# Four seed loads of ple_gate's second product, moved in the SyncE queue from six pieces ahead of their use to just behind the loads of its first blocks

## The chip, the cores and the metric

The kernel runs on one core of one Trainium2 chip. The metric is the time of one execution on the device, in microseconds (us). Before the change it is 787.4 us, the median of three runs (786.9 to 788.35 us). The times of single instructions below come from one further execution, taken by the hardware profiler.

## The reference

One layer of a transformer trunk, in float32: a windowed attention with a gate, an output projection, a gated embedding, and a norm. With DEPTH = 1 only the first of four mixers runs. In the words of the reference, shortened:

```python
hn = rmsnorm(x, norm_g[0])                      # x is 512 x 2048
q, k, v, gate = split(hn @ w_in)                # widths 2048, 256, 256, 2048
scores = q k^T / 8 + bias, masked to a window of 128
probs = softmax(scores with one sink for each head)
y = ((probs @ v) * silu(gate)) @ w_out          # 2048 x 2048
x = x + y
emb = p[0] @ ple_proj[0]                        # 256 -> 2048
g = sigmoid(rmsnorm(x, ple_norm[0]) @ ple_gate[0])   # 2048 x 2048
x = x + emb * g
return rmsnorm(x, final_g)
```

## The kernel before

**Number format.** Each float32 operand is split into a high part, rounded to the format float32r, and a low part, the rest. A product is three matmuls: high times high, high times low, low times high (lines 126 to 128, `mm3`).

**Stages.** Up to about 451 us the kernel makes q, k, v, the gates and the attention. Then come two products with a 2048 x 2048 matrix each: `w_out`, and after it `ple_gate`, from about 621 us on. Each is done as a scheme of Strassen's kind: six large products of half-sized blocks, in the order 1, 7, 6, 5, 3, 4 (`ORDER_PLE`), and a seventh, number 2, done one level deeper as seven small products that are put between the pieces of the large ones. Some of these products take sums of weight blocks. For the numbers 7 and 5 of `ple_gate` such sums were written to HBM during the attention, and they are loaded from there.

**Pieces.** All weights of the two products come as a list of pieces (`Pieces`, line 725), 128 x 1024 in float32, 512 KB each, numbered in the order in which TensorE uses them. Piece 71 is the first of `ple_gate`. Its product 1 takes the pieces 71 to 74 (first half) and 75, 76, 78, 79 (second half), with the small pieces 77 and 80 between them. Its second product, number 7, takes the pieces 81, 82, 84, 85 (first half) and 88, 90, 92, 93 (second half), with the small pieces 83, 86, 87, 89, 91 and 94 between them. TensorE needs 12 matmuls for a large piece and 6 for a small one. A step here means the work on one piece.

**Kinds of pieces.** The eight pieces of product 7 are *seeds*: each is loaded into one of eight tiles named `grown`. Product 6 uses these tiles after another block was added to each by an accumulating DMA on the GpSimd queue (line 739), and product 4 uses them after a second such addition. An addition to a tile is issued when the tile was split for the product before. All other pieces are loaded by SyncE (line 752) into tiles named `braw`, whose rooms are: the eight `grown` rooms for the pieces from `w_out`'s product 6 to its end (piece 70), then three rooms `wraw` and one `fourth`, taken in turns. A room comes free when its piece was split.

**Split and use.** A piece is split by ScalarE (line 760, `bhi`) and VectorE (line 761, `blo`), two steps ahead of its use, into three rooms for the split parts. So the split of a piece waits until TensorE is done with the piece three before, and it waits for the piece's load.

**The order of loads.** TensorE and SyncE run in the order in which the program is written. At step i, `ahead` (line 774) issues the load of each piece that may be loaded up to there: three ahead for `braw` before piece 71, five ahead where they take `grown` rooms, four ahead from step 71 on, and six ahead for a seed:

```python
for n in range(max(i, 0), min(i + 6, last) + 1):
    kind = self.specs[n][0]
    if n not in self.base and n >= self.done and kind not in ("grow", "emb") and (kind == "seed" or n <= i + (...)):
        self._prepare(n)
```

If a load has to wait for its room, all that SyncE has behind it waits too.

**Turning x.** Between the two products x is turned, for a part by DMAs on the GpSimd queue: `turn_blocks` writes blocks to HBM (`apart<-blocks`, line 1064), `gather_blocks` reads them back (`s<-apart`, line 1072), and ScalarE scales what came back (`hT`, line 1081).

Of the kernel before, what the change touches and what calls it, by code (L numbers as in the profile page):

```python
# [55 lines left out]
def trunk_kernel(ctx: ExitStack, tc: tile.TileContext, a: dict):  # L56
# [31 lines left out]
    class Weights:  # L88


        def __init__(self, ahead):
            self.srcs, self.ahead, self.raw, self.made = [], ahead, [], []

            self.todo, self.asked, self.apart = [], 0, False
# [104 lines left out]
    for k in range(KC):  # L199
# [45 lines left out]
        if k == 0:  # L245
            first, second = slice(0, 1), slice(1, 2)
# [154 lines left out]
    for b in range(exact, BUCKETS):  # L401
        d = np.nonzero(bk == b)[0]
        if len(d):
            lo, n = P - 1 + int(d.min()), len(d)
# [281 lines left out]
    def block(nm, r, c, jj, m):  # L686

        r = r if nm == "w_out" else 3 - r
        return a[nm][2 * (c - 1) + jj, 4 * (r - 1) + m]
# [35 lines left out]
    class Pieces:  # L725
# [48 lines left out]
        def ahead(self, i):  # L774

            last = len(self.specs) - 9
            for n in range(max(i, 0), min(i + 6, last) + 1):
                kind = self.specs[n][0]
                if n not in self.base and n >= self.done and kind not in ("grow", "emb") and (kind == "seed" or n <= i + (5 if far_from <= n < far_to else 4 if i >= far_to else 3)):
                    self._prepare(n)  # L780
            while self.done <= min(i + 2, last):
                self._split(self.done)
                self.done += 1
# [14 lines left out]
    B = Pieces()  # L798

    def add_stage(nm, order):  # L800
        at = {}

        for p in order:
            for jj in range(2):
                at[p, jj] = []
                for m in range(4):
                    at[p, jj].append(len(B.specs))
                    if (nm, p) in SUMS:
                        src = summed[nm, p, jj, m]
                    else:  # L810
                        src = block(nm, *{1: (1, 1), 3: (2, 2), 6: (1, 1), 4: (2, 1)}[p], jj, m)
                    growing = () if nm == "w_out" else (7, 6, 4)
                    kind = "one" if p not in growing else "seed" if p == growing[0] else "grow"
                    B.add(kind, src, (nm, jj, m) if p in growing else None)
                    if nm == "w_out" and (p, jj, m) in EMBED_AT:
                        at.setdefault("embed", []).append(len(B.specs))
                        B.add("emb", None)
                    for q in SMALL[nm].get((p, jj), {}).get(m, ()):
                        v = at.setdefault(("small", q), [])
                        src = summed.get(("small", nm, q, len(v)))  # L820
                        if src is None:
                            src = small_block(nm, *{1: (1, 1), 2: (2, 1), 3: (2, 2)}[q], len(v))
                        v.append(len(B.specs))
                        B.add("one", src)
        return at
# [8 lines left out]
    at_out = add_stage("w_out", ORDER_OUT)  # L834
    at_ple = add_stage("ple_gate", ORDER_PLE)

    far_from, far_to = at_out[6, 0][0], at_ple[ORDER_PLE[0], 0][0]

    class Forms:
# [850 lines left out]
    first = block(0, 0)  # L1690
# [44 lines left out]
    n = done[3]  # L1735
# [81 lines left out]
```

## Time and profile before

| what | before |
|---|---|
| median of three runs | 787.4 us (786.9 to 788.35) |
| time of the profiled execution | 788.12 us |
| its span, first to last instruction | 786.4 us |
| TensorE (PE) busy | 774.0 us, 98% of the span |
| VectorE (DVE) busy | 617.8 us, 79% |
| ScalarE (ACT) busy | 528.5 us, 67% |
| DMA queue q1 (SyncE's loads) | 154.58 MB, 56.1% of 16 engines |
| DMA queue q0 (GpSimd's, with the additions) | 57.74 MB, 35.0% |

Times inside the span count from its start. In a timeline row the first number is the start, the second the duration, and what stands in brackets is the engine's idle time before and what ended it. `SPq` is SyncE issuing a DMA. In a row of DMA issues, the last number is the median time from issue to landing. Matmul starts follow each other every 0.227 us when nothing is in the way, and their ends overlap, so starts are compared and not ends. In a row of a window, the columns are the length, then busy time and number of instructions of PE, PEld, DVE, ACT and POOL, then the granted TensorE clock, the busy share of the 16 DMA engines, and what they moved in GB/s.

### The profile page before, as it was taken

How to read it: one execution, taken by the hardware profiler on the slowest of the kernel's cores; microseconds unless marked ns; L12 is line 12 of the kernel's file. 1: busy time of each engine (PE TensorE's matmuls, PEld its weight loads, DVE VectorE, ACT ScalarE, POOL GpSimd, SP SyncE). 2: the span in 40 equal slices, each digit the busy share in tenths (PEclk: the TensorE clock that was granted, in tenths of full speed). 3: DMA queues.
4: the chain of work that ended last, by engine and by line, in shares of the span. 5: the costliest groups of instructions: out<-in, count | busy, mean ns of one | idle time of the engine just before them, and what ended most of it. 6: DMA issues, size and time to landing. Idle time of an engine off the chain costs nothing.

```text
span 786.4 us, 11143 instructions
## 1 busy us (share of the span) xinstructions
PE 774.0 (98%) x3652; PEld 645.6 (82%) x3652; DVE 617.8 (79%) x1069; ACT 528.5 (67%) x1121; POOL 167.2 (21%) x303
## 2 busy tenths in 40 slices
PE   9999999999999999999999999999999999999995
PEld 8888888888888888888888888888888888777884
DVE  4546697877877688877878899976899889878995
ACT  6643586766767676766666654678766888846974
POOL 0201523122222314132322200001111211221111
PEclk9999999999999999999999999999999999999998
DMA  9988899999999989999998589869799699999966
GB/s 347 291 209 298 184 276 303 293 279 269 278 257 271 270 240 287 267 293 256 290 255 206 142 319 329 274 208 309 260 366 335 210 354 287 276 279 282 328 145 215
DMA packets 52410, 213.02 MB, mean 271 GB/s; under 512 B 7984, under 2 KB 9008, under 8 KB 46592
## 3 DMA queue, kind: packets, MB, share of 16 engines
q1 hardware_dynamic: 39152, 154.58, 56.1%
q0 software_dynamic: 13200, 57.74, 35.0%
q8 instruction: 29, 0.48, 0.2%
q14 instruction: 29, 0.24, 0.1%
HBM read 195.45 MB, written 78.69 MB: 349 GB/s over the span
## 4 chain that ended last, share of the span: by engine, by line
PE 88%; DMA 4%; DVE 3%; issue 2%; ACT 2%; POOL 0%; POOLq 0%; DVEq 0%; ACTq 0%
PE gps L126 7%; PE gps L127 7%; PE gps L128 7%; PE qps L126 7%; PE qps L128 7%; PE qps L127 7%; PE o L128 6%; PE o L126 6%; PE o L127 6%; PE g L127 2%; PE s L485 2%; DMA braw<-in_ple_gate 2%; PE g L128 2%; PE g L126 2%; DMA braw<-ple_gate 2%
## 5 line engine op out<-in xcount | busy, mean ns | idle before, releaser
L761 DVE TENSOR_TENSOR blo<-braw,bhi 128x1024 fp32r<-128x1024 f32 x100 | 121.3, 1218 | 29.1 <-ACT bhi L760 28.3
L760 ACT CAST bhi<-braw 128x1024 fp32r<-128x1024 f32 x100 | 105.0, 1051 | 52.6 <-PE o L128 19.6
L126 PE MATMUL gps<-xh,whi 128*128 128x512 f32 x256 | 100.0, 390 | 0.0
L127 PE MATMUL gps<-xl,whi 128*128 128x512 f32 x256 | 100.0, 390 | 0.0
L128 PE MATMUL gps<-xh,wlo 128*128 128x512 f32 x256 | 99.8, 390 | 0.0
L126 PE MATMUL qps<-xh,whi 128*128 128x512 f32 x224 | 87.8, 392 | 0.0
L128 PE MATMUL qps<-xh,wlo 128*128 128x512 f32 x224 | 87.5, 390 | 0.0
L127 PE MATMUL qps<-xl,whi 128*128 128x512 f32 x224 | 87.4, 390 | 0.0
L575 POOL TENSOR_SCALAR_AFFINE_SELECT own<-r 64x512 fp32r<-64x512 f32 (+1 forms) x48 | 32.5, 677 | 238.4 <-DVE r L565 234.5
L110 DVE TENSOR_TENSOR wlo<-wraw,whi 128x1024 fp32r<-128x1024 f32 x60 | 73.5, 1226 | 3.2 <-ACT whi L109 3.1
L126 PE MATMUL o<-bhi,fho 128*128 128x512 f32 x192 | 74.8, 390 | 0.0
L127 PE MATMUL o<-blo,fho 128*128 128x512 f32 x192 | 74.7, 389 | 0.0
L128 PE MATMUL o<-bhi,flo 128*128 128x512 f32 x192 | 74.7, 389 | 0.0
L109 ACT CAST whi<-wraw 128x1024 fp32r<-128x1024 f32 x60 | 62.4, 1040 | 5.1 <-issue 4.1
L127 PE MATMUL g<-blo,fhg 128*128 128x512 f32 x160 | 63.5, 397 | 1.7 <-DVE blo L761 1.7
L126 PE MATMUL g<-bhi,fhg 128*128 128x512 f32 x160 | 63.1, 394 | 0.9 <-ACT bhi L760 0.9
L128 PE MATMUL g<-bhi,flg 128*128 128x512 f32 x160 | 62.9, 393 | 0.0
L128 PEld LDWEIGHTS gps<-xh,wlo 128*128 128x128 f32 x256 | 48.1, 188 | 10.2
L126 PEld LDWEIGHTS gps<-xh,whi 128*128 128x128 f32 x256 | 48.1, 188 | 9.2
L529 ACT ACTIVATE t<-t,sm 128x129 f32<-128x129 f32 (+1 forms) x128 | 49.6, 389 | 8.6 <-DVE sm L525 7.4
L127 PEld LDWEIGHTS gps<-xl,whi 128*128 128x128 f32 x256 | 48.1, 188 | 8.9
L564 ACT CAST r<-pt 128x256 fp32r<-128x256 f32 x56 | 20.9, 372 | 50.0 <-PE pt L551 49.5
(297 smaller groups left out, 1830.0 us busy)
## 6 DMA issues: line engine op xcount, KB each, us to landing
wraw<-in_w_gate_in SPq DMA_DIRECT2D x32, 512.0 KB, 8.1
w_out<-in_w_out POOLq DMA_DIRECT2D x32, 512.0 KB, 9.0
braw<-w_out SPq DMA_DIRECT2D x32, 512.0 KB, 6.1
wraw<-in_w_q SPq DMA_DIRECT2D x28, 512.0 KB, 6.5
braw<-in_w_out SPq DMA_DIRECT2D x22, 512.0 KB, 5.9
braw<-in_ple_gate SPq DMA_DIRECT2D x22, 512.0 KB, 6.4
xw<-in_first SPq DMA_DIRECT2D x14, 640.5 KB, 6.6
w_out<-in_w_out SPq DMA_DIRECT2D x16, 512.0 KB, 10.2
```

The source lines that it names most:

```text
L109: nc.scalar.copy(hi, raw)
L110: nc.vector.tensor_sub(lo, raw, hi.bitcast(F32))
L126: nc.tensor.matmul(ps, sh, mh, start=first, stop=False, skip_group_check=more)
L127: nc.tensor.matmul(ps, sh, ml, start=False, stop=False, skip_group_check=more)
L128: nc.tensor.matmul(ps, sl, mh, start=False, stop=last, skip_group_check=more)
L485: nc.tensor.matmul(s_ps[:, u, : 2 * n], st, of_keys[:, first * 2 * QB : (first * QB + n) * 2], start=True, stop=True)
L529: nc.scalar.activation(su, su, AF.Exp, bias=sm[:, u : u + 1], accum_out=sm[:, 2 + u : 3 + u])
L564: nc.scalar.copy(rh, src)
L575: nc.gpsimd.affine_select(out=flat(own), in_=flat(r).bitcast(F32), pattern=[[0, 8], [sign, HB]], compare_op=ALU.is_ge, fill=0.0, base=-HB ...
L760: nc.scalar.copy(hi[:, :n], raw)
L761: nc.vector.tensor_sub(lo[:, :n], raw, hi[:, :n].bitcast(F32))
```

## The change

Four of the eight seeds, the pieces 81, 82, 84 and 85, are now loaded at the steps 67, 68, 69 and 70, one at each. They were loaded at the steps 75, 76, 78 and 79. No load is added or removed, and every other engine's order stays as it was.

```diff
@@ Pieces.ahead @@
                 if n not in self.base and n >= self.done and kind not in ("grow", "emb") and (...):
                     self._prepare(n)
+            first = at_ple[ORDER_PLE[0], 0][0] - 4
+            if first <= i < first + 4 and seeds[i - first] not in self.base:
+                self._prepare(seeds[i - first])
             while self.done <= min(i + 2, last):
                 self._split(self.done)
                 self.done += 1
@@ after add_stage @@
     at_out = add_stage("w_out", ORDER_OUT)
     at_ple = add_stage("ple_gate", ORDER_PLE)
 
+    seeds = [n for n, (kind, _, _) in enumerate(B.specs) if kind == "seed"]
     far_from, far_to = at_out[6, 0][0], at_ple[ORDER_PLE[0], 0][0]
```

SyncE's queue at the end of `w_out`, before (the number behind `braw` or `grown` is the piece's; in brackets stand the semaphores it waits for, where DVE means that a split must have freed its room):

```order
L752 DMA braw70_6449<-w_out_4_1_3_811 128x1024 [waits DMAHW0_49,DVE_49]
L752 DMA braw71_6497<-in_ple_gate 128x1024 [waits DMAHW1_49]
L752 DMA braw72_6509<-in_ple_gate 128x1024 [waits DMAHW2_49,DVE_49]
L752 DMA braw73_6556<-in_ple_gate 128x1024 [waits DMAHW3_49]
L752 DMA braw74_6604<-in_ple_gate 128x1024 [waits DMAHW4_49]
L752 DMA braw75_6606<-in_ple_gate 128x1024 [waits DMAHW5_49,DMAHW1_49,DVE_49]
```

The same place in the changed kernel:

```order
L752 DMA braw70_6449<-w_out_4_1_3_811 128x1024 [waits DMAHW0_49,DVE_49]
L752 DMA grown81_6471<-ple_gate_7_0_0_814 128x1024 [waits DMAHW1_49,DVE_49]
L752 DMA braw71_6499<-in_ple_gate 128x1024 [waits DMAHW2_49]
L752 DMA grown82_6501<-ple_gate_7_0_1_815 128x1024 [waits DMAHW3_49,DVE_49]
L752 DMA braw72_6513<-in_ple_gate 128x1024 [waits DMAHW4_49]
L752 DMA grown84_6515<-ple_gate_7_0_2_816 128x1024 [waits DMAHW5_49,DVE_49]
L752 DMA braw73_6562<-in_ple_gate 128x1024 [waits DMAHW6_49]
L752 DMA grown85_6564<-ple_gate_7_0_3_817 128x1024 [waits DMAHW7_49,DVE_49]
L752 DMA braw74_6612<-in_ple_gate 128x1024 [waits DMAHW0_49]
L752 DMA braw75_6614<-in_ple_gate 128x1024 [waits DMAHW2_49,DMAHW1_49,DVE_49]
```

Each of the four seeds stands ahead of one of the pieces 71 to 74 and waits for a split: its room is that of piece 63, 64, 65 or 66.

SyncE's queue in `ple_gate`'s first product, before:

```order
L752 DMA braw79_6707<-in_ple_gate 128x1024 [waits DMAHW5_49,DVE_49]
L752 DMA grown81_6709<-ple_gate_7_0_0_814 128x1024
L752 DMA braw80_6739<-in_ple_gate 128x1024 [waits DMAHW6_49,DVE_49]
L752 DMA grown82_6741<-ple_gate_7_0_1_815 128x1024
L752 DMA grown84_6778<-ple_gate_7_0_2_816 128x1024
L752 DMA braw83_6809<-small_ple_gate_7_0_812 128x1024 [waits DMAHW7_49,DVE_49]
L752 DMA grown85_6811<-ple_gate_7_0_3_817 128x1024
L752 DMA braw86_6870<-small_ple_gate_7_1_813 128x1024 [waits DMAHW0_49,DVE_49]
L752 DMA grown88_6872<-ple_gate_7_1_0_818 128x1024 [waits DMAHW1_49,DMASW2_49]
```

The same place in the changed kernel:

```order
L752 DMA braw79_6715<-in_ple_gate 128x1024 [waits DMAHW5_49,DMAHW1_49,DVE_49]
L752 DMA braw80_6745<-in_ple_gate 128x1024 [waits DMAHW2_49,DVE_49]
L752 DMA braw83_6811<-small_ple_gate_7_0_812 128x1024 [waits DMAHW7_49,DMAHW3_49,DVE_49]
L752 DMA braw86_6870<-small_ple_gate_7_1_813 128x1024 [waits DMAHW4_49,DVE_49]
L752 DMA grown88_6872<-ple_gate_7_1_0_818 128x1024 [waits DMASW2_49]
```

Four loads are gone from between the pieces 79 and 86; from piece 86 on the order is the same in both kernels.

## The prediction

> **What bounds the kernel now.** I read the busy shares first (TensorE 98% of the span), then windows of time, to find where TensorE is not full, then the timelines of TensorE and ScalarE there, and last the DMA issues that these wait for. From the table of windows:
>
> ```profile
> 613.00:617.00 4.00, 4.00 (x19) 3.25 (x19) 4.00 (x5) 3.67 (x6) 1.99 (x4) 1.00 0.17 53
> 650.00:670.00 20.00, 20.00 (x90) 16.57 (x89) 18.32 (x22) 16.39 (x26) 4.26 (x5) 1.00 1.06 279
> 700.00:710.00 10.00, 8.38 (x35) 6.39 (x34) 5.01 (x6) 3.27 (x4) 1.21 (x3) 0.97 1.05 276
> 706.50:713.00 6.50, 4.88 (x13) 3.50 (x13) 3.65 (x4) 3.29 (x4) 1.76 (x2) 0.74 1.05 290
> 710.00:720.00 10.00, 9.02 (x34) 6.96 (x34) 6.70 (x8) 4.43 (x5) 1.69 (x2) 0.85 1.04 321
> ```
>
> TensorE does 90 matmuls in the 20 us from 650, so 45 in 10 us, but 35 and 34 in the two stretches from 700 to 720: 21 fewer, at 0.227 us 4.8 us. VectorE and ScalarE are slack there. The DMA engines are full from 650 to 720, and nearly idle (0.17) from 613 to 617. TensorE's own rows:
>
> ```profile
> 706.30 0.39 PE L128 MATMUL smallg<-bhi,small_alg 128*128 128x512 f32 x1
> 707.56 0.51 PE L126 MATMUL g<-bhi,fhg 128*128 128x512 f32 x1 [0.87 <-ACT bhi L760]
> 708.82 0.50 PE L127 MATMUL g<-blo,fhg 128*128 128x512 f32 x1 [0.75 <-DVE blo L761]
> ...
> 718.50 0.39 PE L126 MATMUL g<-bhi,fhg 128*128 128x512 f32 x1
> 719.87 0.50 PE L127 MATMUL g<-blo,fhg 128*128 128x512 f32 x1 [0.98 <-DVE blo L761]
> ```
>
> The first stall is at piece 109, the first of product 5: TensorE waits for its high part, then for its low part. ScalarE's rows say why:
>
> ```profile
> 706.46 1.05 ACT L760 CAST bhi<-braw 128x1024 fp32r<-128x1024 f32 x1 [5.48 <-DMA braw<-ple_gate]
> ...
> 713.45 1.05 ACT L760 CAST bhi<-braw 128x1024 fp32r<-128x1024 f32 x1 [2.14 <-DMA braw<-ple_gate]
> 715.02 1.05 ACT L760 CAST bhi<-braw 128x1024 fp32r<-128x1024 f32 x1 [0.53 <-DMA braw<-ple_gate]
> ```
>
> ScalarE stood ready 5.48 us before piece 109 landed; the rows at 713.45 and 715.02 are the pieces 111 and 112. So loads bound this place. Their issues, and the landing of four of them (the pieces 83, 92, 94 and 109, in this order):
>
> ```profile
> 634.86 0.32 SPq L752 DMA_DIRECT2D braw<-small_ple_gate  x1
> 643.01 0.32 SPq L752 DMA_DIRECT2D grown<-ple_gate  x1
> 655.37 0.33 SPq L752 DMA_DIRECT2D braw<-in_ple_gate  x1
> 657.96 17.46 SPq L752 DMA_DIRECT2D braw<-small_ple_gate  x4
> 675.61 0.32 SPq L1443 DMA_DIRECT2D e<-embeds  x1
> 679.23 5.47 SPq L752 DMA_DIRECT2D braw<-in_ple_gate  x2
> 684.81 0.43 SPq L1443 DMA_DIRECT2D e<-embeds  x1
> 689.32 23.59 SPq L752 DMA_DIRECT2D braw<-ple_gate  x6
> ```
>
> ```profile
> braw<-small_ple_gate SPq DMA_DIRECT2D x1, 512.0 KB, 10.7
> grown<-ple_gate SPq DMA_DIRECT2D x1, 512.0 KB, 18.2
> braw<-in_ple_gate SPq DMA_DIRECT2D x1, 512.0 KB, 17.3
> braw<-ple_gate SPq DMA_DIRECT2D x1, 512.0 KB, 17.0
> ```
>
> Piece 83 lands at 634.86 + 10.7 = 645.6, piece 92 at 661.2, piece 94 at 672.7, piece 109 at 706.3. The lag grows from 10.7 to 18.2 us between 635 and 643, and then holds: 17.3 at 655, 17.0 at 689. From piece 94 to piece 109 nine loads land (four small ones, two e, two of line 752, and 109) in 33.6 us, 3.73 us each, and they are issued in 689.32 - 655.37 = 34.0 us, 3.77 each. As much comes in as goes out, so a lag that is there at 650 is still there at 700. The share of the two queues, for 650 to 702 and below it for 630 to 646:
>
> ```profile
> q0 software_dynamic: 1914, 6.99, 67.3%
> q1 hardware_dynamic: 2042, 7.46, 38.1%
> ...
> q1 hardware_dynamic: 1246, 4.55, 79.1%
> ```
>
> From 650 on the additions on q0 hold 67% of the engines, and SyncE's q1 moves 7.46 MB in 52 us, 143 GB/s. From 630 to 646 it moved 4.55 MB in 16 us, 284 GB/s, or 1.85 us for a load of 0.524 MB. The lag is made where many loads are issued at once, four of the moved seeds among them, just ahead of the time when q1 falls to half its pace.
>
> **The change part by part.** Work of TensorE, ScalarE, VectorE and GpSimd is the same, in the same order; 2.1 MB of loads move.
>
> *What goes.* The stalls that late loads make. Piece 109: two gaps of 707.56 - 706.30 and 708.82 - 707.56, 1.26 each, less the rhythm of 0.227, together 2.06 us. The half clock behind it: in the window 706.5 to 713 the granted clock is 0.74, so 0.26 x 6.5 = 1.7 us. The gap at 718.50: 1.37 - 0.23 = 1.14 us; here piece 112's low part waited behind other work of VectorE that the late loads had pressed together. The sum is 4.9 us, against 4.8 by the count of matmuls.
>
> [...]
>
> *Is the relief enough?* A piece is in time if its cast starts 2.05 us before TensorE wants it (1.05 for `bhi`, 1.22 for `blo`, less 0.227 since `blo` is wanted one matmul later). The durations:
>
> ```profile
> L761 DVE TENSOR_TENSOR blo<-braw,bhi 128x1024 fp32r<-128x1024 f32 x100 | 121.3, 1218 | 29.1 <-ACT bhi L760 28.3
> ```
>
> Without a stall TensorE would want piece 109 at 706.53 and the next ones every 12 x 0.227 = 2.73 us, so their casts must start at 704.5, 707.2, 709.9 and 712.7. They came 2.0 (109), 3.5 (111) and 2.3 us (112) late. The relief has to be 3.5 us.
>
> Four loads at 1.85 us are 7.4 us of q1's time. The shortest landings, with an empty queue, are those of three loads issued between 626 and 632:
>
> ```profile
> braw<-in_ple_gate SPq DMA_DIRECT2D x3, 512.0 KB, 5.9
> ```
>
> The lower end: of piece 83's 10.7 us only 10.7 - 5.9 = 4.8 are queue, and no more can be gained there. With the seeds gone q1 then has the pieces 80 and 83 alone in the 8 us from 630 to 638; two loads at 1.85 and the gather, taken as a third, are 5.6, so 2.4 us of the gain are spent idle, and 2.4 stay. The upper end: the loads that are left land before q0's additions begin. The pieces 86, 88, 87, 90, 89 and 92 stand in line behind 83; if 86, issued at about 637.8, lands 5.9 us later at 643.7, the five others follow at 1.85, and 92 lands at 652.9, not 661.2: 8.3 us. I take the upper end less what a short dry spell costs: twelve loads from 92 to 109 at 3.73 would end at 697.7, but piece 103 is issued only at 675.1, when the queue ahead of it is just empty, and so 109 lands at about 699.7, a relief of 6.6 us. Then 110, 111 and 112 land at 703.4, 707.1 and 710.9. All are in time, by 4.8, 3.8, 2.8 and 1.8 us. The upper end is nearer since the lag held for 34 us in the trace.
>
> *What is added.* The four seeds stand at SyncE's queue ahead of the pieces 71 to 74, and wait for the splits of the pieces 63 to 66. What there is of that place (the landings are those of 71 and 74):
>
> ```profile
> 599.42 31.16 SPq L752 DMA_DIRECT2D braw<-in_ple_gate  x9
> ```
>
> ```profile
> braw<-in_ple_gate SPq DMA_DIRECT2D x1, 512.0 KB, 8.6
> braw<-in_ple_gate SPq DMA_DIRECT2D x1, 512.0 KB, 13.7
> ```
>
> ```profile
> 604.60 2.58 DVE L761 TENSOR_TENSOR blo<-braw,bhi 128x1024 fp32r<-128x1024 f32 x2
> ```
>
> ```profile
> 614.39 1.06 ACT L760 CAST bhi<-braw 128x1024 fp32r<-128x1024 f32 x1 [0.30 <-PE smallo L128]
> ...
> 620.04 1.06 ACT L760 CAST bhi<-braw 128x1024 fp32r<-128x1024 f32 x1
> ...
> 623.65 2.01 ACT L760 CAST bhi<-braw 128x1024 fp32r<-128x1024 f32 x2
> 630.73 1.71 ACT L1081 ACTIVATE hT<-s,pn 128x256 f32<-128x256 f32 x4
> ```
>
> The split of piece 66 ends at 604.60 + 2.58 = 607.2, so piece 74 is issued at about 607.6 and not at 601.1. Before, 71 landed at 599.4 + 8.6 = 608.0 and 74 at 601.1 + 13.7 = 614.8: three loads in 6.8 us, 2.27 each. From 605.8 on, eight loads at that pace put 71 (the second) at 610.3, 72 at 614.9, 73 at 619.4 and 74 at 624.0; their casts are at 614.39, 620.04, 623.65 and 624.6. All in time: the cost is nothing, covered by the engines' idle time from 613 to 617, and if that cover were gone it would be the last rival's price. On GpSimd's queue the read-back of turned blocks runs at that time:
>
> ```profile
> 614.57 0.56 POOL L1072 DMA_DIRECT2D s<-apart  x1 [10.08 <-DMA apart<-blocks]
> ```
>
> ScalarE scales it at 630.73, some 16 us later; sharing the engines with two or three loads (5 to 7 us) does not reach that far.
>
> *Sum.* The profiled execution took 788.12 us (span 786.4, with 1.7 around it), and 788.12 - 4.9 = 783.2. It lies 0.7 above the median of 787.4, and 787.4 - 4.9 = 782.5. Since the stall and its half clock can differ between executions, I forecast a value between: **782.7 us**, 0.6% faster.
>
> **The rivals.** *Relief too small.* With the lower end, 2.4 us, piece 109 lands at 703.9, 110 at 707.6 and 111 at 711.4, so 111 is 1.5 us late, and the clock may fall behind it or not: 1.5 to 3.2 of the 4.9 us stay, 2.4 on the mean. For it: q1 has little to do at 630 to 638 once the seeds are gone. Against it: the lag of 17 us held. It gives 787.4 - 2.5 = **784.9**.
>
> *The lag comes back.* The queue loads a fixed number of pieces ahead; if the lag regrows between 650 and 689 whatever it was, piece 109 is as late as before. For it: the engines are full for 70 us in any case, and the change takes no byte away. Against it: issue every 3.77 us, landing every 3.73, so nothing regrows. No change, **787.4**.
>
> *The half clock is not the stall's.* If the clock falls at this place for another reason, only 3.2 of the 4.9 us go: **784.2**. Against it: the clock is 1.00 from 650 to 670, and it falls just behind the stall. [...]
>
> *The seeds hold up ple_gate's start (slower).* Eight loads must land in place of four, in a time when q0 also moves turned blocks. If q1 got there what it gets from 650 on, 3.73 us a load, 74 would land at 605.8 + 8 x 3.73 = 635.6. TensorE's first matmul of piece 71, in the chain of waits, is at 621.57:
>
> ```profile
> 621.57 0.23 PE g L126
> ```
>
> It wants piece 74 three steps of 2.73 later, at 629.8, and its cast at 627.7: a stall of 7.9 us, with a half clock of 1.7 behind it, against a gain of 4.9: 787.4 + 4.7 = **792.1**. It decides from (627.7 - 605.8) / 8 = 2.74 us a load; the trace has 2.27 there.
>
> **How the numbers follow.** The forecast has 0.70, its own range 781.3 to 784.1 (a stall of 4.9 with 0.5 either way, and executions that differ by 0.7). Relief too small 0.12, the clock 0.04, the lag comes back 0.07, slower 0.07. The range that leaves out 2 in 10 takes in the forecast, the clock and most of the small relief: 781.2 to 785.6. About 0.2%, 1.6 us, is what a measurement can tell from no change; faster by more is the first case, the clock and nearly all of the small relief, 0.84; within it 0.09; slower 0.07.
>
> **What would show it.** In the changed kernel's profile: seeds issued between 601 and 608; a DMA share well above 0.17 from 613 to 617; piece 92 landing some 10 us after its issue and not 18.2; no cast in the 700s that waits over 2 us for a load; 45 matmuls in each 10 us from 700 to 720 at a granted clock of 1.00. I am wrong if piece 109 still lands 15 us after its issue, or if a cast between 614 and 628 waits for a load.

## The result, and the profile after

The changed kernel takes **781.81 us** (median of six runs, 781.46 to 783.11), against 788.18 us (786.9 to 788.58) for the kernel before, measured beside it: a ratio of 0.9924, 95% interval 0.9911 to 0.9937. Measured again later, beside other runs of the kernel before, it took 782.91 us against 787.32, a ratio of 0.9950 (0.9934 to 0.9966). So the gain is 6.4 us the first time and 4.4 us the second. The forecast was 782.7. The profiled execution took 782.2 us with a span of 780.5; before, 788.12 and 786.4.

The windows of before again, and one of 50 us, with the same columns.

```profile
613.00:617.00 4.00, 4.00 (x23) 3.36 (x22) 3.49 (x5) 3.20 (x7) 1.68 (x4) 1.00 1.02 412
650.00:700.00 50.00, 50.00 (x222) 41.44 (x221) 46.94 (x55) 38.78 (x56) 12.74 (x15) 1.00 1.06 274
700.00:710.00 10.00, 10.00 (x46) 8.29 (x45) 5.87 (x7) 4.40 (x5) 2.50 (x3) 1.00 1.05 274
710.00:720.00 10.00, 9.70 (x44) 7.65 (x43) 9.46 (x12) 7.72 (x12) 1.73 (x2) 1.00 1.06 349
```

The idle DMA engines from 613 to 617 are in use now (1.02 for 0.17), TensorE does 46 and 44 matmuls in the stretches where it did 35 and 34, and the clock is 1.00 in all four rows. The kernel before has in its 50 us:

```profile
650.00:700.00 50.00, 49.97 (x219) 40.52 (x218) 45.58 (x54) 38.23 (x57) 12.32 (x14) 1.00 1.06 278
```

Three matmuls fewer, 0.68 us: there was a small stall ahead of 700, too, which the prediction had not counted. It is spread over stretched gaps between matmul starts from 671 to 677 (0.74 us by the starts), around this cast of the kernel before, which waited for a load (piece 94):

```profile
672.76 1.05 ACT L760 CAST bhi<-braw 128x1024 fp32r<-128x1024 f32 x1 [2.01 <-DMA braw<-in_ple_gate]
```

SyncE's queue after the change, first the first and the last of the four moved seeds, then the issues of the pieces 83 (with 86), 92, 94 and 109:

```profile
601.12 0.32 SPq L752 DMA_DIRECT2D grown<-ple_gate  x1
...
606.55 0.32 SPq L752 DMA_DIRECT2D grown<-ple_gate  x1
...
634.20 3.26 SPq L752 DMA_DIRECT2D braw<-small_ple_gate  x2
641.35 0.44 SPq L752 DMA_DIRECT2D grown<-ple_gate  x1
654.71 0.33 SPq L752 DMA_DIRECT2D braw<-in_ple_gate  x1
687.22 0.33 SPq L752 DMA_DIRECT2D braw<-ple_gate  x1
```

From issue to landing the pieces 83, 92, 94 and 109 took, in this order (before: 10.7, 18.2, 17.3, 17.0):

```profile
braw<-small_ple_gate SPq DMA_DIRECT2D x1, 512.0 KB, 5.4
grown<-ple_gate SPq DMA_DIRECT2D x1, 512.0 KB, 10.8
braw<-in_ple_gate SPq DMA_DIRECT2D x1, 512.0 KB, 10.3
braw<-ple_gate SPq DMA_DIRECT2D x1, 512.0 KB, 12.6
```

Piece 109 lands at 687.22 + 12.6 = 699.8, where it landed at 706.3. The next two are cast as they land, 111 at 707.50 and 112 at 711.30. ScalarE, and TensorE where the one gap is left:

```profile
707.50 1.05 ACT L760 CAST bhi<-braw 128x1024 fp32r<-128x1024 f32 x1 [2.52 <-DMA braw<-ple_gate]
711.30 1.05 ACT L760 CAST bhi<-braw 128x1024 fp32r<-128x1024 f32 x1 [2.75 <-DMA braw<-ple_gate]
```

```profile
713.24 0.39 PE L126 MATMUL g<-bhi,fhg 128*128 128x512 f32 x1
713.93 0.50 PE L127 MATMUL g<-blo,fhg 128*128 128x512 f32 x1 [0.30 <-DVE blo L761]
```

ScalarE still waits 2.5 us and more for the pieces 111 and 112. TensorE loses only 0.69 - 0.23 = 0.46 us by it. The line of the chain of waits, after and before:

```profile
PE 94%; DVE 2%; DMA 1%; issue 1%; ACT 0%; POOL 0%; POOLq 0%; DVEq 0%; ACTq 0%
```

```profile
PE 88%; DMA 4%; DVE 3%; issue 2%; ACT 2%; POOL 0%; POOLq 0%; DVEq 0%; ACTq 0%
```

DMA falls from 4% to 1%. Of the 5.9 us between the two profiled executions, the stall at piece 109 is 2.06, the half clock 1.7, the gap of piece 112 1.14 - 0.46 = 0.68, the small stall ahead of 700 0.68. Another 0.66 is no doing of the change. It stands between the two executions from the first 7 us of the span on, and is still 0.66 at this matmul, after and before:

```profile
617.05 0.48 PE L126 MATMUL o<-bhi,fho 128*128 128x512 f32 x1
```

```profile
617.71 0.48 PE L126 MATMUL o<-bhi,fho 128*128 128x512 f32 x1
```

### The profile page after: what moved, and what is told of

It is laid out like the page before. It is cut to its first block, busy times and chain, and to the rows that moved or that the text cites. A ratio compares the mean times of both kernels' runs of the same rounds, so it can differ in the third digit from the quotient of the medians.

```text
span 780.5 us, 11140 instructions
## 1 busy us (share of the span) xinstructions
PE 770.5 (99%) x3652; PEld 644.0 (83%) x3652; DVE 618.4 (79%) x1069; ACT 529.0 (68%) x1121; POOL 167.4 (21%) x303
## 4 chain that ended last, share of the span: by engine, by line
PE 94%; DVE 2%; DMA 1%; issue 1%; ACT 0%; POOL 0%; POOLq 0%; DVEq 0%; ACTq 0%
PE gps L126 7%; PE gps L127 7%; PE gps L128 7%; PE qps L126 7%; PE qps L128 7%; PE qps L127 7%; PE o L126 6%; PE o L127 6%; PE o L128 6%; PE g L127 4%; PE g L128 4%; PE g L126 4%; PE s L485 2%; PE vps L290 2%; PE o L603 2%; PE pt L551 2%
## 5 line engine op out<-in xcount | busy, mean ns | idle before, releaser
L128 PEld LDWEIGHTS gps<-xh,wlo 128*128 128x128 f32 x256 | 48.1, 188 | 10.3
```

What stands on the lines that cost most here:

```text
L128: nc.tensor.matmul(ps, sl, mh, start=False, stop=last, skip_group_check=more)
```

## The experiments

The theory: what a load costs depends on when it is in SyncE's queue. Four loads fewer there before the additions begin at about 650 shorten the line by several us, and from 650 on the lag is held. The rivals: that the additions have no part in holding it; that the early place has a worth of its own, whichever loads are put there; that the relief goes evenly with the number of loads. The first diff is against the kernel before, all others against the changed kernel. "The 700s" are 700 to 720 us. The experiments were timed in three sittings, each on a chip of its own and each with its own runs of the kernel before, so the ratios are what to compare.

| moved | ratio to before | 95% interval |
|---|---|---|
| 81, 82 | 0.9983 | 0.9969 to 0.9997 |
| 84, 85 | 0.9957 | 0.9939 to 0.9976 |
| 84, 85 (81, 82 behind 80) | 0.9951 | 0.9937 to 0.9965 |
| 81, 82, 84, 85 (the change) | 0.9924, again 0.9950 | 0.9911 to 0.9937, 0.9934 to 0.9966 |
| the same, at steps 71 to 74 | 0.9974 | 0.9962 to 0.9985 |
| 84, 85, 88, 90 | 0.9965 | 0.9952 to 0.9978 |
| 88, 90, 92, 93 | 0.9947 | 0.9933 to 0.9962 |
| first five | 0.9934 | 0.9922 to 0.9946 |
| first six | 0.9963 | 0.9948 to 0.9978 |
| all eight | 0.9980 | 0.9970 to 0.9991 |
| none, additions later | 1.0020 | 1.0010 to 1.0030 |

### Later additions

```diff
-                    self.due.append((i + (2 if self.specs[i][0] == "seed" else 3), n))
+                    late = at_ple[5, 0][0] + (n - at_ple[4, 0][0])
+                    self.due.append((i + 2 if self.specs[i][0] == "seed" else max(i + 3, late), n))
```

The second additions, those for product 4, come in product 5.

> The kernel before, with no seed moved; the second addition to each seed's tile, which product 4 alone needs, is issued at the steps 109 to 116 and not three steps after product 6 used the tile (677 to 702 us). Theory (the additions on q0 take two thirds of the engines and hold q1 at half its pace): from 677 us on q1 moves 280 GB/s or more, the lag of 17 us is gone by 695, piece 109 is in time and the half clock with the stall is gone; the additions then run beside the loads of product 3 and may make a new, smaller stall there: 782 to 785.5 us. Rival (q1's lag has nothing to do with the additions, the engines are simply full): piece 109 as late as before, 787 to 789.

Measured: 789.04 us against 787.45, not the 782 to 785.5 expected. The queues from 678 to 690 and the landing of piece 109; then the 700s, the stretch from 730 to 742, and ScalarE there:

```profile
q1 hardware_dynamic: 861, 3.10, 69.2%
q0 software_dynamic: 154, 0.54, 22.6%
...
braw<-ple_gate SPq DMA_DIRECT2D x1, 512.0 KB, 4.4
```

```profile
700.00:720.00 20.00, 20.00 (x90) 16.57 (x89) 16.93 (x19) 12.40 (x18) 6.76 (x8) 1.00 0.93 266
730.00:742.00 12.00, 9.37 (x34) 7.06 (x34) 6.06 (x8) 6.44 (x9) 1.12 (x2) 0.86 1.07 286
```

```profile
734.61 1.04 ACT L760 CAST bhi<-braw 128x1024 fp32r<-128x1024 f32 x1 [5.33 <-DMA braw<-in_ple_gate]
```

With q0 at 23%, q1 moves 3.10 MB in 12 us, 258 GB/s; in the kernel before q0 holds 68% in the same 12 us and q1 moves 1.66 MB, 138 GB/s. The lag was still 16.0 us at piece 94, issued at 656 ahead of the additions that were moved, and is 4.4 us at piece 109 instead of 17.0, with no load moved. The stall of the 700s is gone. So the additions hold the lag. The kernel is not faster, because the additions now meet the loads of product 3, where such a stall comes up at 733 with a half clock behind it (the last two rows: ScalarE waits 5.33 us for a load). The place that was tried for the additions has no time to spare; no other was tried.

### Two seeds, 81 and 82

```diff
-            if first <= i < first + 4 and seeds[i - first] not in self.base:
+            if first <= i < first + 2 and seeds[i - first] not in self.base:
```

> Only the seeds 81 and 82 are loaded early; 84 and 85 stay six pieces ahead. Theory (the lag of SyncE's queue q1 at 650 us, carried on to piece 109): half the load off the queue is about half of the relief, some 3 us of the 6.6; piece 109 lands at about 703 us, in time, the pieces 111 and 112 some 1 to 2 us late, so part of the stall stays: 783 to 785.5 us, between before and the change. Rival (the early seeds work by being early, and all four or none matter; or a threshold at the clock): 781.8 or 788.

Measured: 785.89 us against 787.45, with a wide spread (782.93 to 788.0 in ten runs), a little above the 783 to 785.5 expected. The landing of the pieces 83 and 92, and TensorE at piece 109 and behind it:

```profile
braw<-small_ple_gate SPq DMA_DIRECT2D x1, 512.0 KB, 7.4
...
grown<-ple_gate SPq DMA_DIRECT2D x1, 512.0 KB, 19.5
```

```profile
705.84 0.39 PE L128 MATMUL smallg<-bhi,small_alg 128*128 128x512 f32 x1
707.02 0.50 PE L126 MATMUL g<-bhi,fhg 128*128 128x512 f32 x1 [0.80 <-ACT bhi L760]
708.28 0.51 PE L127 MATMUL g<-blo,fhg 128*128 128x512 f32 x1 [0.76 <-DVE blo L761]
...
712.12 0.50 PE L127 MATMUL g<-blo,fhg 128*128 128x512 f32 x1 [0.76 <-DVE blo L761]
```

Piece 83 lands 3.8 us earlier than before (634.34 + 7.4 = 641.7 for 645.5), two loads at 1.9, but piece 92 is as late as ever (19.5 us for 18.2), and the stall at 109 stands (it landed at 705.9, not at the 703 expected). The gain was lost between the landings of 83 and 86 (641.7 and 647.5), when the queue landed two loads in 5.8 us beside the gather on q0. That the gather slowed them is argued: no run moved it. If loads counted evenly, two would be worth half of what four are; the profile shows almost no relief at 109. The ratio alone does not rule it out: half the gain would be 0.9962 by the first measurement of the change and 0.9975 by the second, and the interval here is 0.9969 to 0.9997.

### Two seeds, 84 and 85

```diff
-            if first <= i < first + 4 and seeds[i - first] not in self.base:
-                self._prepare(seeds[i - first])
+            if first <= i < first + 2 and seeds[2 + i - first] not in self.base:
+                self._prepare(seeds[2 + i - first])
```

> Only the seeds 84 and 85 are moved to the steps 67 and 68; 81 and 82 stay at 75 and 76. Theory of the count: two loads less in SyncE's queue are worth what 81 and 82 were worth in the run of two, so about 785.9 us, piece 92 landing 19 us after its issue. Theory of the place: with 81 and 82 gone piece 83 landed 3.8 us earlier, but the gain was spent between 641.7 and 647.5, where the queue moved two loads in 5.8 us beside the gather; 84 and 85 stand at the place where the line is already long, so without them the line stays shorter to the end: piece 92 lands under 15 us after its issue, the stall at piece 109 is at most 1.2 us, and the time is 782 to 784 us. [...]

Measured: 782.54 us against 786.81 (five runs, 781.79 to 784.8). Piece 92 takes 13.8 us to land, inside what was expected by the place:

```profile
grown<-ple_gate SPq DMA_DIRECT2D x1, 512.0 KB, 13.8
```

Two other loads, and the median gains 4.3 us instead of 1.6; the intervals of the two ratios overlap by a little (0.9969 to 0.9976). Of the stall in the 700s this execution had kept 0.7 and 1.2 us, at other pieces, and a new one came at 645, where ScalarE had waited for the pieces 79 and 80:

```profile
637.30 1.05 ACT L760 CAST bhi<-braw 128x1024 fp32r<-128x1024 f32 x1 [0.96 <-DMA braw<-in_ple_gate]
639.85 1.06 ACT L760 CAST bhi<-braw 128x1024 fp32r<-128x1024 f32 x1 [1.50 <-DMA braw<-in_ple_gate]
```

### Piece 80 ahead of 81

As the last, and the seeds 81 and 82 loaded five pieces ahead instead of six:

```diff
-... and (kind == "seed" or n <= i + (5 if ...)):
+... and ((kind == "seed" and (n > seeds[1] or n <= i + 5)) or n <= i + (5 if ...)):
```

> The seeds 84 and 85 early, as in the run of the middle two, and the seeds 81 and 82 loaded five pieces ahead of their use instead of six, so that piece 80 stands ahead of 81 in SyncE's queue. If it was the seed 81 ahead of piece 80 that made ScalarE wait 1.50 us for piece 80 at 639.85 and TensorE 1.03 us at 645.15, both are gone, piece 80 lands about 1.3 us earlier, and the time is 1.0 us under that of the middle two: ratio 0.9945, level with the changed kernel within 1 us. If that stall has another cause, the ratio stays at 0.9957.

Measured: 783.34 us against 787.32, ratio 0.9951. The casts at that place wait for no load any more, and the new stall at 645 is gone:

```profile
637.33 1.05 ACT L760 CAST bhi<-braw 128x1024 fp32r<-128x1024 f32 x1 [0.92 <-PE g L128]
638.69 1.06 ACT L760 CAST bhi<-braw 128x1024 fp32r<-128x1024 f32 x1 [0.30 <-PE smallg L128]
```

So it was the order of 80 and 81 (or of 82, which moved with 81). What it is worth in time (1.0 us was expected, the ratios differ by 0.5 us) lies within the measurement, and this execution, the slowest of its five, lost 0.9 us more in the 700s than the last.

### The middle four, and the last four

The middle four are the seeds 84, 85, 88 and 90; the last four, with a 4 for the 2 of `seeds[2 + i - first]` below, 88, 90, 92 and 93:

```diff
-            if first <= i < first + 4 and seeds[i - first] not in self.base:
-                self._prepare(seeds[i - first])
+            if first <= i < first + 4 and seeds[2 + i - first] not in self.base:
+                self._prepare(seeds[2 + i - first])
```

> The other four seeds, 88, 90, 92 and 93, take the early places; 81, 82, 84 and 85 are loaded six pieces ahead as before. Theory (bytes off q1 before the additions begin, whichever seeds they are): these four landed before at 649 to 669 us, the last two at 3.8 us each, so leaving them out there relieves at least as much: piece 94 lands at about 661 us and not 672.7, piece 109 at 696 to 700; the stall of the 700s goes wholly, 781 to 782 us. Rival (what counts is that the first seeds of product 7 are there early, which the split then finds sooner): no gain, 787 to 788.5.

> The seeds 84, 85, 88 and 90 are moved to the steps 67 to 70; 81, 82, 92 and 93 stay. Theory (bytes out of the crowd, whichever seeds): as much relief as with the last four or the first four, no stall at 706 to 718. What differs is the cost ahead of it: the casts of the pieces 78 to 82 wait for loads since 81 and 82 stand between 79 and 80, as with the last four, whose stall at 645 cost 1.2 us; but there 84 and 85 were in line too. I expect at most 0.6 us of stall at 645 and 781.5 to 783.0 us. If it shows 785 or more, it is the first two that count.

Measured: 783.18 us against 787.45 for the last four, 784.02 against 786.81 for the middle four. The last four, 781 to 782 us expected, took most of the lag away (piece 109 lands 9.1 us after its issue) and the stall of the 700s with it:

```profile
700.00:720.00 20.00, 20.00 (x90) 16.57 (x89) 17.18 (x20) 13.23 (x19) 4.36 (x5) 1.00 1.05 310
```

They paid for it at 645, with the seed 81 still in line ahead of piece 80, as with 84 and 85:

```profile
645.48 0.50 PE L126 MATMUL g<-bhi,fhg 128*128 128x512 f32 x1
646.74 0.50 PE L127 MATMUL g<-blo,fhg 128*128 128x512 f32 x1 [0.76 <-DVE blo L761]
```

So no virtue lies in the first four or in the order that the change gives them: each of the three sets of four that were moved relieves the line. The middle four miss what I expected: 784.0, not 781.5 to 783.0, with 0.9 us of stall at 645 and 0.8 at 714.35. They do not gain over 84 and 85 alone. Their queue landed only one load from 644.8 to 649.3 beside the gather, so there, too, a part of the gain was lost in that spell; why this spell was slower than in other executions stays open.

### Eight seeds, six, five

```diff
-            if first <= i < first + 4 and seeds[i - first] not in self.base:
+            if first <= i < first + 8 and seeds[i - first] not in self.base:
```

and the same with 6 and 5.

> All eight seeds are loaded early, one at each of the steps 67 to 74. Theory: the lag at 650 us falls to next to nothing (piece 94 lands within 8 us of its issue), the 0.6 us that the change leaves at piece 112 goes too, 781 to 781.8 us. Rival (the cover from 613 to 630 us is used up by four loads, and eight hold up the pieces 75 to 80): a cast between 620 and 640 us waits for its load, TensorE stalls there, 783 to 790.

> The first six seeds (81, 82, 84, 85, 88, 90) at the steps 67 to 72. Eight of them held up the pieces 76 to 80 and cost two stalls at 637 to 654; four cost nothing. The two more are issued ahead of the pieces 75 and 76. If the cost begins where the idle engines from 613 to 617 (4 us, two to three loads) are used up, six stall TensorE by about 1 us at 637 to 654 and gain the last 0.6 us at 713: 781.5 to 783.5 us. If it grows evenly from four to eight, 783.8.

> The changed kernel with a fifth seed, piece 88, moved as well, to step 71, ahead of piece 75. The one gap that was left in the 700s (0.57 us from 713.24 on) should go, since piece 92 and what follows land 1.3 us earlier. Against it: six seeds stalled TensorE by 1.0 us at 646. If the cost ahead begins only where the pieces 78 to 80 land late, five stand between, and the time is within 0.5 us of the changed kernel, more likely above it than below.

Measured: eight 785.86 us against 787.45, six 783.6 against 786.81, five 782.23 against 787.32. With eight the rival came true and not the theory (781 to 781.8 us); six lie just above the 783.5 of an abrupt cost and level with the 783.8 of an even one, so the two cannot be told apart. ScalarE with eight, in the slowest of its ten executions:

```profile
630.03 1.05 ACT L760 CAST bhi<-braw 128x1024 fp32r<-128x1024 f32 x1 [1.91 <-DMA braw<-in_ple_gate]
...
636.02 1.05 ACT L760 CAST bhi<-braw 128x1024 fp32r<-128x1024 f32 x1 [3.33 <-DMA braw<-in_ple_gate]
...
645.07 1.05 ACT L760 CAST bhi<-braw 128x1024 fp32r<-128x1024 f32 x1 [1.87 <-DMA braw<-in_ple_gate]
```

TensorE with eight, from 636 to 655, and in the 700s:

```profile
636.00:655.00 19.00, 14.75 (x55) 10.48 (x54) 13.62 (x15) 14.94 (x25) 3.99 (x6) 0.91 0.80 254
700.00:720.00 20.00, 20.00 (x90) 16.57 (x89) 18.04 (x21) 11.96 (x14) 4.37 (x5) 1.00 1.06 276
```

The 700s are clean, but TensorE idles 4.2 of the 19 us and has a half clock as well: the eight hold up the pieces 76 to 80. This is the mechanism of the slower rival, seeds that hold up the start of `ple_gate`; in these traces four cost nothing, five 0.4 us of stall at 645.62, six 1.0 us at 646, and eight most of the gain (0.9980). Five (0.9934) cannot be told from the four of the change (0.9950 beside them on the same chip, 0.9924 before), and nothing that was run beats the change by more than the intervals.

### The same four, later

The four seeds 81, 82, 84 and 85 at the steps 71 to 74:

```diff
-            first = at_ple[ORDER_PLE[0], 0][0] - 4
+            first = at_ple[ORDER_PLE[0], 0][0]
```

> The same four seeds 81, 82, 84 and 85, but moved to the steps 71 to 74 only, where SyncE issues them at about 617 to 628 and the DMA engines are at 0.67 to 0.93, not at the steps 67 to 70, ahead of the idle time from 613 to 617. If only the order before the additions counts, the relief is as in the changed kernel, 782 us. If the idle time is what pays for the four loads, they hold up the pieces 75 to 80 by up to 4 x 1.85 = 7.4 us, casts between 626 and 645 wait for loads by more than 2 us, and the time is 784 to 787 us. I expect the second, about 784.5.

Measured: 784.65 us against 786.81 (seven runs, 782.88 to 785.71), about what I expected. The profiled execution is the fastest of them, with the 700s clean and a stall of 0.9 us at 645.83. The DMA engines are left idle from 613 to 617 as before, and a cast at 629.84 waits for a load:

```profile
613.00:617.00 4.00, 4.00 (x20) 3.28 (x19) 4.00 (x5) 3.67 (x6) 2.73 (x5) 1.00 0.25 81
```

```profile
629.84 1.05 ACT L760 CAST bhi<-braw 128x1024 fp32r<-128x1024 f32 x1 [1.73 <-DMA braw<-in_ple_gate]
```

The order ahead of the additions gives the relief; that the idle time at 613 is what keeps it free of cost fits these rows. But the profile shows only 0.9 us of cost, and no cast from 626 to 645 waited over the 2 us expected; what the rest of the median is made of stays open, since the slower executions have no profile.

### The change again

> The changed kernel itself, unaltered, beside the next two on one chip: 0.9924 of the time before, 0.9911 to 0.9937. It shows whether four seeds are still ahead of two (0.9957) where both are measured together with the same runs of before; if the two seeds 84 and 85 carry the whole gain, the difference is under 1 us.

Measured: 782.91 us against 787.32, six runs from 781.81 to 785.88. In this execution the gap of piece 112 is gone too, and piece 92 lands 7.2 us after its issue, not 10.8:

```profile
700.00:720.00 20.00, 20.00 (x90) 16.57 (x89) 16.94 (x19) 13.30 (x19) 4.35 (x5) 1.00 1.06 313
```

```profile
grown<-ple_gate SPq DMA_DIRECT2D x1, 512.0 KB, 7.2
```

One program, two executions, and the lag at 650 differs by 3.6 us, about the worth of two loads. That is as large as what separates the lists of moved seeds, so one profile of each does not rank them.

In the same sitting the seeds 84 and 85 alone, with 80 ahead of 81, took 783.34 us: a ratio of 0.9951 beside the 0.9950 of the change. So two of the four loads, in the right order, cannot be told from all four. That the other two add anything is not shown.

## Why the prediction was right

**The bound.** Right. Loads bound the 700s, as late pieces and not as slow engines; in each run where piece 109 landed before 703, TensorE had no stall at it.

**The relief.** Right, and within 0.3 us in the execution profiled first: I put the pieces 109 to 112 at 699.7, 703.4, 707.1 and 710.9; 109 landed at 699.8, 111 and 112 are cast at 707.50 and 711.30, at once as they land. Part of this is luck. Piece 92 landed at 652.1 there (predicted 652.9) and at 641.59 + 7.2 = 648.8 the second time. The way there was not quite as reckoned: piece 86 landed at 641.6, 2.1 us before its 643.7, and the five loads behind it took 2.1 us each and not 1.85. Of the bounds I gave for the relief (2.4 and 8.3 us), the mechanism of the lower one, seeds that leave only idle time behind, was not seen; where gain was lost, with 81 and 82, it went into loads that landed slowly.

**The size.** The forecast gain was 4.7 us, from 787.4. Measured were 6.4 us, from 788.18, and 4.4 us, from 787.32. That the first time lies 0.9 us from the forecast says little about the terms of the sum.

**Which loads.** Here the prediction knew less than it seemed. It priced four equal loads at 1.85 us each. The runs with two speak for 84 and 85 carrying the gain (0.9957, and 0.9951 with 80 ahead of 81) and 81 and 82 little of it (0.9983). That the line is set by what happens after 640, beside the gather, stands in the "gather, taken as a third" of the lower end, but not in the value I took.

**That the lag holds.** Right, and now tested rather than read: with the additions moved, q1 went at 258 GB/s and the lag fell to 4.4 us. The lag of the changed kernel, 10.8 us at piece 92, 10.3 at 94 and 12.6 at 109, did not grow back to 17 either. The rival that the lag comes back is out.

**The sum.** The term of the gap at 718.50 was taken whole at 1.14 us; 0.46 of it stayed in one execution and none in the other. The step that failed there is the margin of 1.8 us for piece 112: I had set its need by the time of the kernel before, but TensorE came 0.66 + 0.68 us earlier, the piece landed 0.4 later, and VectorE began its low part 0.3 us behind the cast, after other work. The small stall from 671 to 677, 0.68 us, was missing from the sum: the cast that waited 2.01 us for a load at 672.76 belongs to the same lag, and I had read the timeline only from 700. The two errors nearly cancel.

**The early place.** Right for four. The pieces 71 to 74 were reckoned at 610.3, 614.9, 619.4 and 624.0 and landed at 608.9, 614.8, 617.2 and 621.9, and no cast at 613 to 624 waited for a load. From the first seed (606.5) to piece 74 a load took (621.9 - 606.5) / 7 = 2.2 us, below the 2.74 that I named as the point from which it decides. With more loads ahead of them the pieces behind do come late, as the pieces 76 to 80 with eight seeds show.

**No cast that waits over 2 us.** Wrong, as a sign to look for. Two casts wait 2.52 and 2.75 us in the changed kernel, at no cost or 0.46 us, since ScalarE is free and stands ready two pieces ahead. The idle time of an engine that waits early says nothing by itself; the matmul starts do.

**The half clock.** It came with the stall, but its 1.7 us should not have been a term of their own. With the stall gone the clock is 1.00 there, and in two other traces a half clock comes behind another stall: at 651 with eight seeds, where stalls of 1.7 and 1.0 us end at 650.37 and 651.63, and at 736 with later additions, where one of 2.0 us ends at 735.70. But not behind each: with 81 and 82 alone the stall of 2.0 us stood and the clock was 1.00 from 700 to 720. The rival of 784.2 us is out; why one stall has a half clock behind it and another of nearly its length has none was not shown.

What a half clock is worth can be read from the mean granted clock of every timed execution. One of 3.41 us takes 0.0022 off the mean; the one at the end of the span, 5.2 us long in the trace of before and 5.0 in that of the change, takes off 0.0033 and 0.0032. The profiled executions with a half clock ahead of the end have means of 0.995 (before) and 0.994 (later additions, eight seeds); the other ten, in none of which one was seen, have 0.996 to 0.998. So I read a mean of 0.995 or less as a half clock besides the one at the end, and a mean of 0.997 or more as none; this is an estimate from those thirteen. Of the 48 executions of the kernel before that were timed beside the experiments, 17 have 0.995 or less and 22 have 0.997 or more, and on the mean their times lie 0.1 and 0.0 us below the median of their sitting. By this reading the kernel before lost as much without the half clock as with it. (With eight seeds it is otherwise: the two executions at 0.994 are the slowest, 788.18 and 789.33 us against at most 786.3.) The likely reason is that piece 111 was 3.5 us late by the prediction's own working: where the stall at 109 is 2 us and no half clock follows, TensorE waits for the next pieces instead, as with 81 and 82, where TensorE lost another 1.00 us ahead of 712.12 and 1.21 us ahead of 719.02. The 4.9 us stand as what late loads cost in one execution, but the terms cover for one another.

## What to carry to other kernels

When transfers are late, ask where the lag was made, not where it hurts: here it was made at 640, held for 50 us by a second queue that took two thirds of the engines, and paid at 706. A load taken out of a crowded spell can be worth more than one taken out just ahead of it (here 84 and 85 against 81 and 82), and the stretch that takes it in has room for a few only (four or five here; eight cost most of the gain). And the costs of two late places in a row need not add up: what the first delays, the second may no longer have to wait for. Where two executions of one program differ by as much as the variants do, rank by repeated times and use the profile for the mechanism.

## What the runs showed of the hardware

**The half clock.** In three of the traces TensorE's granted clock is 0.50 for 3.41 us behind a stall: in the kernel before, with later additions, and with eight seeds, in this order. The first row of each is the stretch ahead of the fall, the second the half clock:

```profile
706.09:709.50 3.41, 1.79 (x7) 0.95 (x6) 1.96 (x3) 2.28 (x3) 0.00 (x0) 1.00 1.06 276
709.50:712.91 3.41, 3.41 (x10) 2.63 (x9) 1.70 (x2) 1.04 (x1) 1.76 (x2) 0.50 1.04 298
```

```profile
733.11:736.52 3.41, 1.22 (x5) 0.44 (x3) 0.84 (x1) 1.92 (x3) 0.00 (x0) 1.00 1.05 274
736.52:739.93 3.41, 2.97 (x7) 2.39 (x8) 3.41 (x6) 2.45 (x4) 0.00 (x0) 0.50 1.07 304
```

```profile
647.86:651.27 3.41, 1.49 (x6) 0.66 (x4) 3.25 (x4) 3.41 (x8) 0.00 (x0) 1.00 0.54 205
651.28:654.68 3.40, 3.05 (x7) 2.48 (x8) 3.14 (x4) 3.04 (x5) 1.65 (x2) 0.50 0.32 40
```

And the 700s of the kernel before and of the run with 81 and 82, whose stall at 705.84 was nearly as long as that of the kernel before (2.0 for 2.06 us):

```profile
700.00:720.00 20.00, 17.39 (x68) 13.35 (x67) 11.70 (x14) 7.70 (x9) 2.90 (x4) 0.91 1.05 298
```

```profile
700.00:720.00 20.00, 16.64 (x69) 12.37 (x68) 12.08 (x14) 8.09 (x11) 2.63 (x3) 1.00 1.00 282
```

So of two stalls of nearly the same length one has a half clock behind it and the other has none, and the two executions do 68 and 69 matmuls in the 20 us. What decides whether the clock falls was not shown.

The half clock does not explain the spread of 5 us of the run with 81 and 82: seven of its ten executions have a mean clock of 0.997, by the reading above no half clock but the one at the end, and they reach from 782.93 to 788.0 us. What makes that spread stays open.

**Two queues, equal packets.** From 650 to 702, q0 and q1 of the kernel before move nearly the same number of packets (1914 and 2042; from 678 to 690, 446 and 458), but q0's, most of them of the additions (14 of 512 KB), hold the engines 67.3% of the time and q1's 38.1%. A plain load of 512 KB takes 3.73 us there, and 1.85 us from 630 to 646, with the gather beside it but no additions.
